# Four weight-tile subtractions of a two-layer hybrid model, on VectorE instead of GpSimd

## The chip, the cores and the metric

The kernel runs on one core of one Trainium2 chip. The core has a tensor engine (TensorE, PE in the profile, with its weight loads as PEld), VectorE (DVE), ScalarE (ACT), GpSimd (POOL) and SyncE (SP), which here issues the DMAs. Each engine works through its own queue in order and waits on semaphores for what the others produce. The metric is device time of one execution in microseconds (us); less is better.

## What is computed

Two layers over 512 tokens of width 1024, batch 1, in fp32. Each layer normalises its input, projects it, mixes it in three ways (a recurrent mix of RWKV type, a gated linear recurrence, and attention on compressed latents), gates the three results and adds their projection to the residual. A norm closes the whole.

```python
h = x
for l in range(DEPTH):                      # 2
    xn = rms_norm(h, ln_g[l])
    proj = xn @ w_in[l]
    u_a, z_a, u_b, z_b, q_lat, kv_lat, k_rope, z_c = jnp.split(proj, pts, axis=-1)
    y_a = rwkv7_mix(u_a, ...)
    y_b = rms_norm(rglru_mix(u_b, ...), lru_out_g[l])
    y_c = rms_norm(mla_mix(q_lat, kv_lat, k_rope, ...), mla_out_g[l])
    y = jnp.concatenate([y_a * silu(z_a), y_b * silu(z_b), y_c * silu(z_c)], axis=-1)
    h = h + y @ w_out[l]
return rms_norm(h, final_g)
```

## The kernel before

**Products in three parts.** A product of fp32 matrices is made of three products of numbers that TensorE takes in one pass (type fp32r). Each operand is split into a high part H, which is a copy rounded to fp32r, and a low part L, which is the operand less H. `mm3` (lines 232 to 234) then adds up H times H, L times H and H times L. So every tile of weights passes through `weights` (L217): a DMA brings it into a `wr` buffer (three of them), ScalarE copies it to H (`wH`, four buffers; the copy is in the helper at L141), and one engine subtracts to give L (`wL`, four buffers; L228). L228 reads two operands from SBUF, `wr` and `wH`. A `wr` buffer is free for the next load when its subtraction is done.

**Which engine subtracts.** A counter `wn` goes up by one per weight tile, over the whole kernel. VectorE takes the tile when the counter divides by `wmod`, GpSimd takes all others. `wmod` is set stage by stage: 5 at the head of a layer (WD, L491), then 1000, 2 and 2. In the first layer the tiles numbered 1 to 4 therefore go to GpSimd, and number 5 to VectorE.

**What the first four tiles are.** The projection's columns are cut into 29 blocks of 128, and a block's weights come in two halves of 128x512. The first product of a layer is block 12, the second block 0, and both are made in two halves of 256 tokens each, so that the first half can start before all rows are normalised (`proj` with `halves`, L330). Tiles 1 and 2 are the halves of block 12, tiles 3 and 4 those of block 0. The raw data of the first three is loaded ahead by the list `LO` (L64); the fourth takes the `wr` buffer that the first leaves.

**The norm beside it.** At the start, four tiles of 128 rows are normalised (`norm_tile`, L287). For each: ScalarE squares and sums the rows (L241), VectorE adds the two sums (L245), ScalarE takes the logarithm and the exponential for a first inverse root (L138), and VectorE refines it in three small steps on 128x1 operands (L253, L254, L255). Then for each half of the columns VectorE scales rows and gains (L297), TensorE transposes four blocks into PSUM (L302), ScalarE copies them out as the high part xH (L141), and VectorE subtracts for the low part xL (L305). The first products need xH and xL of row tiles 0 and 1.

**What sets the order.** The queues' order is not written out: a planner goes through the traced instructions, simulates the engines, and gives each engine the earliest traced instruction that is ready. The norm of all four row tiles is traced ahead of the weights of block 12. Two things are fixed by hand: the list `behind` (L1101) puts the copies to H of tiles 1 and 2 behind the last xH copy of row tile 0, and those of tiles 3 and 4 behind that of row tile 1; and three small VectorE operations (L1104 to L1106) come behind the last xL.

Later in a layer, L498 mixes each projected block with its shifted self, L552 and L562 belong to the chain of decays of the recurrent mix (L562 once for each of four column groups), L524 and L525 are the sums over heads in it, L285 and L300 are the norm's steps in the second layer, and L508 splits two small weights on GpSimd.

Of the kernel before, what the change touches and what calls it, by code (L numbers as in the profile page):

```python
# [12 lines left out]
ALU = mybir.AluOpType  # L13
# [34 lines left out]
def body(ctx, tc, x, wc, wl, wo, w2a2, gagx, wuq, wukv, vec, ln_g, fin_g, cst, out, depth=DEPTH):  # L48
    nc = tc.nc
    V, A, G = nc.vector, nc.scalar, nc.gpsimd  # L50
# [17 lines left out]
    def tl(tag, shape, dt=F32, bufs=1):  # L68
        cnt[0] += 1
        return SB.tile(list(shape), dt, tag=tag, name=f"{tag}_{cnt[0]}", bufs=bufs)  # L70
# [69 lines left out]
    def copy(out, in_, **kw):  # L140
        i = A.activation(out=out, in_=in_, func=AF.Copy, **kw)  # L141
        return getattr(i, "ins", i)
# [63 lines left out]
    def f(ap):  # L206
        return ap.bitcast(F32)
# [6 lines left out]
    wn = [0]  # L214
    wmod = [4]

    def weights(src, n=512, raw=None):  # L217

        if raw is None:
            raw = tl("wr", [128, n], F32, bufs=3)  # L220
            nc.sync.dma_start(out=raw, in_=src)
        H = tl("wH", [128, n], F32R, bufs=4)
        L = tl("wL", [128, n], F32R, bufs=4)
        wn[0] += 1
        i = copy(H, raw)
        if behind:
            tc.add_manual_dep(i, behind.pop(0).name, NOSYNC, reason="issue order")
        (V if wn[0] % wmod[0] == 0 else G).tensor_tensor(out=L, in0=raw, in1=f(H), op=ALU.subtract)  # L228
        return H, L

    def mm3(o, a, b, start, stop):
# [88 lines left out]
    def one_layer(l):  # L320
# [9 lines left out]
        def proj(j, halves=False):  # L330

            if halves:
                o = acc()
                W = [weights(wc[l, j, :, 4 * hf:4 * hf + 4, :].rearrange("p k c -> p (k c)"), raw=raws.pop((j, hf), None)) for hf in range(2)]
                for th in range(2):
                    t = slice(th * 256, (th + 1) * 256)
                    for k in range(8):
                        s = slice((k % 4) * 128, (k % 4 + 1) * 128)
                        w = W[k // 4]
                        mm3(o[:, t], (w[0][:, s], w[1][:, s]), (xH[:, k, t], xL[:, k, t]), k == 0, k == 7)  # L340
                return o
            o, parts = proj_parts(j)
            for part in parts:
                part()
            return o

        def proj_parts(j):
            o = acc()

            def part(hf):  # L350
                H, L = weights(wc[l, j, :, 4 * hf:4 * hf + 4, :].rearrange("p k c -> p (k c)"))
                for k in range(4):
                    s = slice(k * 128, (k + 1) * 128)
                    kk = 4 * hf + k
                    mm3(o, (H[:, s], L[:, s]), xk(kk), kk == 0, kk == 7)

            return o, [lambda: part(0), lambda: part(1)]
# [33 lines left out]
        def out_steps(m, y):  # L391

            W, os = {}, {}

            def step(n, tt, k):
                if tt == 0 and k == 0:
                    W[n] = [weights(wo[l, m, n, :, i, :]) for i in range(4)]
                if k == 0:
                    os[n, tt] = tl("hp", [128, 512], bufs=3), acc()
                    nc.sync.dma_start(out=os[n, tt][0], in_=hsrc[tt, n])  # L400
                hp, o = os[n, tt]
                c = slice(tt * 128, (tt + 1) * 128)
                mm3(o, (y[k][:, 0, c], y[k][:, 1, c]), W[n][k], k == 0, k == 3)
                if k == 3:
                    V.tensor_tensor(out=hp, in0=o, in1=hp, op=ALU.add)
                    hd = spill()
                    nc.sync.dma_start(out=hd, in_=hp)
                    hsrc[tt, n] = hd

            return [lambda n=n, tt=tt, k=k: step(n, tt, k) for n in range(2) for tt in range(4) for k in range(4)]  # L410
# [792 lines left out]
```

## Time and profile before

| | |
|---|---|
| median of 3 runs | 873.0 us (871.79, 873.0, 875.05) |
| the profiled execution | 871.72 us |
| its span in the profile | 869.9 us |
| mean granted TensorE clock | 0.972 of full speed |
| PE, PEld busy | 808.5 us (93%), 624.9 us |
| DVE, ACT, POOL busy | 575.0 us, 493.7 us, 336.1 us |
| DMA | 91.05 MB, mean 105 GB/s |

The span is what the profile covers; the 1.8 us between it and the execution's time lie around it. In rows of the chain of waits a line reads: start in us, duration in us, engine, what is written, line. The chain is followed back from the last instruction, at each step to what released it. In rows of the timeline there follow the operation, output<-input, partitions x elements and type, and the count where like instructions are merged into one row; in brackets stands how long the engine was idle before it and what ended that. In the window table each row is a stretch of the span: its edges and width, then busy time (and instructions) of PE, PEld, DVE, ACT and POOL, the granted clock, the DMA engines' mean share and GB/s. A busy PE is not a PE at its peak, since the ends of matmuls are modelled.

### The profile page before, as it was taken

Reading aid. Unit: us, or ns where it says so; the run is one execution under the profiler, and the core shown is the slowest. Engines: PE = TensorE matmul, PEld = TensorE weight load, DVE = VectorE, ACT = ScalarE, POOL = GpSimd, SP = SyncE. Lnnn points to the kernel's source line nnn. Section 1 sums busy time; section 2 is a strip of 40 time slices with the busy share of each in tenths; the row PEclk is TensorE's granted clock in tenths of the full one; section 3 lists DMA queues with packets and bytes.
Section 4 is the critical chain, followed back from the end, with each engine's and each line's share of the span. In section 5 each row is a group of like instructions: output and inputs, shape, how many; then the busy total and the mean of one; then the engine's idle time right before and its main releaser. Section 6 shows DMA issues by size and latency. Waiting matters only on the chain.

```text
span 869.9 us, 14682 instructions
## 1 busy us (share of the span) xinstructions
PE 808.5 (93%) x5440; PEld 624.9 (72%) x5440; DVE 575.0 (66%) x1169; ACT 493.7 (57%) x980; POOL 336.1 (39%) x303
## 2 busy tenths in 40 slices
PE   3998999998989988999989999999979999899995
PEld 3877878876768867566778788888756787675674
DVE  5687666933656795865484876695265778777736
ACT  5657776356454535564466677844745445365635
POOL 2345357634343342010534656574243423310123
PEclk9997999999899999999989999999999999899998
DMA  6311232420212365213653232333010224731354
GB/s 217 116 62 56 79 108 98 139 75 16 59 33 72 111 215 184 73 57 114 223 177 98 73 98 85 109 108 105 26 42 23 65 86 155 233 109 49 109 170 158
DMA packets 49753, 91.05 MB, mean 105 GB/s; under 512 B 5520, under 2 KB 8336, under 8 KB 49680
## 3 DMA queue, kind: packets, MB, share of 16 engines
q1 hardware_dynamic: 49104, 89.05, 31.8%
q10 hardware_dynamic: 576, 1.05, 0.3%
q8 instruction: 43, 0.70, 0.3%
q14 instruction: 30, 0.25, 0.1%
HBM read 73.30 MB, written 16.78 MB: 104 GB/s over the span
## 4 chain that ended last, share of the span: by engine, by line
PE 70%; DVE 12%; ACT 6%; DMA 4%; issue 4%; POOL 2%; SPq 0%; ACTq 0%; DVEq 0%; POOLq 0%
PE acc L232 16%; PE acc L234 15%; PE acc L233 15%; PE acc L1035 4%; PE ck L1061 3%; PE ps L1053 2%; ACT g L138 2%; PE ps L686 2%; PE ck L827 2%; PE ps L610 1%; ACT UV L141 1%; PE ps L628 1%; DMA dr<-hp 1%; POOL g L701 1%; DMA hp<-in_x_dram 1%
## 5 line engine op out<-in xcount | busy, mean ns | idle before, releaser
L228 POOL TENSOR_TENSOR wL<-wr,wH 128x512 fp32r<-128x512 f32 (+1 forms) x130 | 176.1, 1359 | 296.6 <-ACT wH L141 288.1
L141 ACT ACTIVATE wH<-wr 128x512 fp32r<-128x512 f32 (+1 forms) x192 | 118.9, 622 | 138.9 <-PE acc L233 81.0
L232 PE MATMUL acc<-xH,wH 128*128 128x512 f32 (+1 forms) x496 | 193.5, 391 | 0.0
L234 PE MATMUL acc<-xH,wL 128*128 128x512 f32 (+1 forms) x496 | 192.1, 387 | 0.0
L233 PE MATMUL acc<-xL,wH 128*128 128x512 f32 (+1 forms) x496 | 190.4, 384 | 0.1
L232 PEld LDWEIGHTS acc<-xH,wH 128*128 128x128 f32 x496 | 95.7, 193 | 20.8 <-issue 3.2
L233 PEld LDWEIGHTS acc<-xL,wH 128*128 128x128 f32 x496 | 95.7, 193 | 17.5 <-DVE xL L305 0.6
L234 PEld LDWEIGHTS acc<-xH,wL 128*128 128x128 f32 x496 | 95.3, 192 | 18.0
L232 PE MATMUL acc<-wH,c 128*128 128x512 f32 x192 | 82.7, 431 | 4.2 <-DVE hp L427 4.2
L228 DVE TENSOR_TENSOR wL<-wr,wH 128x512 fp32r<-128x512 f32 (+1 forms) x62 | 51.8, 835 | 50.5 <-ACT wH L141 48.6
L233 PE MATMUL acc<-wL,c 128*128 128x512 f32 x192 | 77.1, 402 | 0.2 <-DVE wL L228 0.2
L234 PE MATMUL acc<-wH,c 128*128 128x512 f32 x192 | 76.4, 400 | 0.0
L141 ACT ACTIVATE UV<-ps 128x512 f32<-128x512 f32 (+4 forms) x88 | 39.3, 478 | 31.0 <-PE ps L1053 22.4
L232 PEld LDWEIGHTS acc<-wH,c 128*128 128x128 f32 x192 | 36.4, 190 | 15.2 <-ACT c L141 3.0
L138 ACT ACTIVATE g<-g 128x512 f32<-128x512 f32 (+1 forms) x58 | 36.4, 628 | 17.5 <-DVE g L704 15.6
L138 ACT ACTIVATE c<-acc,sm 128x128 f32<-128x128 f32 (+3 forms) x64 | 33.5, 526 | 19.3 <-DVE sm L1037 19.1
L1035 PE MATMUL acc<-am,am 128*128 128x128 f32 (+3 forms) x128 | 42.3, 447 | 0.9 <-ACT c L138 0.8
L233 PEld LDWEIGHTS acc<-wL,c 128*128 128x128 f32 x192 | 36.6, 191 | 8.3 <-issue 1.4
L234 PEld LDWEIGHTS acc<-wH,c 128*128 128x128 f32 x192 | 36.5, 190 | 8.4 <-issue 0.5
L141 ACT ACTIVATE c<-g 128x512 fp32r<-128x512 f32 (+1 forms) x40 | 24.3, 628 | 28.9 <-DVE g L958 26.0
L136 ACT ACT_TABLE_LOAD x29 | 37.2, 1283 | 1.2 <-PEq L1191 0.7
L368 POOL TENSOR_TENSOR g<-g,g 128x512 f32<-128x512 f32 x24 | 33.0, 1377 | 12.5 <-ACT g L138 12.5
(217 smaller groups left out, 1602.0 us busy)
## 6 DMA issues: line engine op xcount, KB each, us to landing
wr<-in_wc_dram SPq DMA_DIRECT2D x116, 256.0 KB, 2.7
wr<-in_wo_dram SPq DMA_DIRECT2D x48, 256.0 KB, 3.5
hp<-dr SPq DMA_DIRECT2D x40, 256.0 KB, 3.1
dr<-hp SPq DMA_DIRECT2D x32, 256.0 KB, 3.2
dr<-g SPq DMA_DIRECT2D x16, 256.0 KB, 2.4
g<-dr SPq DMA_DIRECT2D x16, 256.0 KB, 3.6
wr<-in_wl_dram SPq DMA_DIRECT2D x16, 208.0 KB, 2.5
c<-in_x_dram SPq DMA_DIRECT2D x8, 256.0 KB, 6.6
```

The costliest lines, as they stand in the source:

```text
L136: chained(A.preload_act_table_set(SETS[st]))
L138: chained(A.activation(out=out, in_=in_, func=func, **kw))
L141: i = A.activation(out=out, in_=in_, func=AF.Copy, **kw)
L228: (V if wn[0] % wmod[0] == 0 else G).tensor_tensor(out=L, in0=raw, in1=f(H), op=ALU.subtract)
L232: PE.matmul(o, a[0], b[0], start=start, stop=False)
L233: PE.matmul(o, a[0], b[1], start=False, stop=False)
L234: PE.matmul(o, a[1], b[0], start=False, stop=stop)
L368: G.tensor_tensor(out=z, in0=z, in1=s, op=ALU.mult)
L686: PE.matmul(o[hr, :], gw[hr, w, j, :], xc[hr, :], start=True, stop=True)
L827: PE.matmul(to[ur, e, p, :], inv["T"][ur, p * 8 + e * 4 + cp, :], r, start=True, stop=True)
L1035: PE.matmul(o[:, 0:n], qT[:, hd, qt * 128:n], K2[:, p, e, 0:n], start=True, stop=True)
L1061: i = PE.matmul(ot[e * 64:(e + 1) * 64, k2 * 128:T], Vt[:, k2, 2 * p + e, :], PT[:, 2 * (k2 % 2) + e, 0:(4 - k2) * 128], start=(k2 == 0), ...
```

## The change

One condition is added in `weights`: the tiles numbered 1 to 4 are subtracted on VectorE. From the fifth on the rule is as before, and the counter runs on through the second layer, so no other tile changes its engine. The operation, its operands and the rest of the trace are the same.

```diff
         i = copy(H, raw)
         if behind:
             tc.add_manual_dep(i, behind.pop(0).name, NOSYNC, reason="issue order")
-        (V if wn[0] % wmod[0] == 0 else G).tensor_tensor(out=L, in0=raw, in1=f(H), op=ALU.subtract)
+
+        (V if wn[0] % wmod[0] == 0 or wn[0] <= 4 else G).tensor_tensor(out=L, in0=raw, in1=f(H), op=ALU.subtract)
         return H, L
```

## The prediction

> **What bounds the kernel now.** I read the page first, then the chain of waits from 12 to 35 us, then the timeline of GpSimd and VectorE over the same stretch, because the change touches only four instructions there. The page gives the size and shows that the differences on GpSimd are the costliest group by busy time.
>
> ```profile
> span 869.9 us, 14682 instructions
> ...
> L228 POOL TENSOR_TENSOR wL<-wr,wH 128x512 fp32r<-128x512 f32 (+1 forms) x130 | 176.1, 1359 | 296.6 <-ACT wH L141 288.1
> ```
>
> The chain that ended last, while rows 128 to 255 (tile 1) and 256 to 383 (tile 2) are normalised (start, duration):
>
> ```profile
> 12.60 1.25 DVE sm L255
> 13.87 1.72 DVE g L297
> ...
> 19.03 1.27 DVE sm L253
> 20.32 1.21 DVE sm L254
> 21.56 0.17 DVE sm L255
> 21.75 0.76 DVE g L297
> ```
>
> See that L255 on a 128x1 operand takes 1.25 us at 12.60 and 0.17 us at 21.56. The timeline says what stood beside the slow ones: the four differences that the change moves, in two pairs.
>
> ```profile
> 12.54 2.49 POOL L228 TENSOR_TENSOR wL<-wr,wH 128x512 fp32r<-128x512 f32 x2 [11.09 <-ACT wH L141]
> 18.99 2.52 POOL L228 TENSOR_TENSOR wL<-wr,wH 128x512 fp32r<-128x512 f32 x2 [3.96 <-ACT wH L141]
> 29.39 2.61 POOL L508 TENSOR_TENSOR c<-g,c 128x512 fp32r<-128x512 f32 x2 [7.89 <-ACT c L141]
> ```
>
> The first pair ends at about 13.79 and 15.03, the second at about 20.25 and 21.51. VectorE's L255 ends at 13.85, and its first L297 at 15.59, 0.56 after the pair; L253 and L254 end at 20.30 and 21.53. So each slow VectorE instruction waits for a GpSimd difference. Between 15.03 and 29.39 the second pair is all that GpSimd does.
>
> From 22 us on the tensor engine is what ends last (window table: width, busy PE, PEld, DVE, ACT, POOL, granted clock, DMA share, GB/s):
>
> ```profile
> 22.00:28.00 6.00, 5.35 (x45) 5.22 (x45) 4.42 (x11) 3.24 (x6) 0.00 (x0) 1.00 0.45 144
> 28.00:50.00 22.00, 21.99 (x119) 18.56 (x118) 13.24 (x17) 15.18 (x26) 10.67 (x13) 1.00 0.30 97
> ```
>
> It is full from 22.65 to 50, so whatever moment it gets going at is handed down.
>
> **What is removed.** Four stalls on the chain. The clean step of a small operation is 21.56 to 21.75, 0.19 us, and the clean first L297 is the 0.76 segment. The sum: L255 from 12.60 to 13.87 is 1.27, less 0.19, 1.08; the first L297 1.72 less 0.76, 0.96; L253 19.03 to 20.32 is 1.29, less 0.19, 1.10; L254 20.32 to 21.56, 1.24 less 0.19, 1.05. Tile 1 gets 2.04 us, tile 2 2.15 us, together 4.19 us. GpSimd loses 5.0 us of work that nobody else there waits for; its next job, at 29.39, waits for ScalarE.
>
> **What is added.** Four instructions on VectorE, of 0.68 us by the row of 449.22 below. Where they stand in its queue isn't in the trace of before, since the order is a planner's. The nearest rows are in the second layer's norm, where one difference is already on VectorE:
>
> ```profile
> 448.41 0.15 DVE L254 SCALAR_TENSOR_TENSOR sm<-sm,sm 128x1 f32<-128x1 f32 x1
> 448.48 0.68 DVE L285 TENSOR_TENSOR g<-c,c 128x512 f32<-128x512 f32 x1
> 449.08 0.15 DVE L255 SCALAR_TENSOR_TENSOR sm<-sm,sm 128x1 f32<-128x1 f32 x1
> 449.15 0.15 DVE L245 SCALAR_TENSOR_TENSOR sm<-sm 128x1 f32<-128x1 f32 x1
> 449.22 0.68 DVE L228 TENSOR_TENSOR wL<-wr,wH 128x512 fp32r<-128x512 f32 x1
> 449.82 0.87 DVE L300 TENSOR_SCALAR g<-g,sm 128x512 f32<-128x512 f32 x2
> ```
>
> An instruction that is ready is put between two that hang on one another (L285 between L254 and L255, L228 between L255 and L300). L254 to L255 then takes 0.67 instead of 0.19: **an exposed difference costs 0.48 us**. Below it is nothing, where it falls into a wait. The other end is all four exposed, 1.92 us.
>
> When is each ready? ScalarE's copies wH, which they read:
>
> ```profile
> 11.85 1.27 ACT L141 ACTIVATE wH<-wr 128x512 fp32r<-128x512 f32 x2
> ...
> 18.29 0.62 ACT L141 ACTIVATE wH<-wr 128x512 fp32r<-128x512 f32 x1
> ...
> 18.90 0.62 ACT L141 ACTIVATE wH<-wr 128x512 fp32r<-128x512 f32 x1
> ```
>
> The first is ready at 12.48, before L255 would end (12.60 + 0.19 = 12.79): I take it as exposed, behind L255. The second is ready at 13.12, when both L297 (independent of one another) stand ahead of it; it then falls into VectorE's wait for the transposes, free. The third and fourth are ready as tile 2's L253 and L254 run: both exposed.
>
> **The sum.** Tile 1: 2.04 - 0.48 = 1.56 us earlier; so are its transposes, its xH and the first product, which was at 17.50:
>
> ```profile
> 17.50 0.58 PE L232 MATMUL acc<-xH,wH 128*128 128x256 f32 x1
> ...
> 21.38 0.41 PE L232 MATMUL acc<-xH,wH 128*128 128x256 f32 x1
> 21.59 0.33 PE L233 MATMUL acc<-xL,wH 128*128 128x256 f32 x1
> 22.65 0.63 PE L302 MATMUL ps<-C,g 128*128 128x128 f32 x4 [0.72 <-DVE g L297]
> ```
>
> Tile 2: its transposes could start 1.56 + 2.15 - 0.96 = 2.75 us earlier, at 19.90. But 17 products stand ahead of them in the tensor engine's queue, from 17.50 to 21.92. These end 1.56 earlier, at 20.36. So the products become what is late, the idle 0.72 us goes, and the transposes move by 1.56 + 0.72 = **2.3 us**. Two exposed differences in tile 2 are thus covered by 0.46 us of products; if that cover went, the figure is at most 2.75. Bounds from the ordering alone: with the second difference exposed too, 1.80; with the first free too, 2.04 + 0.72 = 2.76.
>
> Behind 22.65 nothing of the norm is changed, and the engine stays full, so I carry 2.3 us to the end. Buffers: freeing a wr buffer lets the next weight load go.
>
> ```profile
> 13.84 8.02 SPq L221 DMA_DIRECT2D wr<-in_wc_dram  x4
> ```
>
> The first of these feeds the fourth copy, wH at 18.90. The first difference now ends at about 13.5 (12.79 + 0.07 + 0.6), against 13.79, so that load isn't later. The second load follows the second difference, which may end later than now; it feeds the fifth copy, behind all of this, and I price it at nothing: the cover is the third and fourth tile's work up to 28 us. The w2a2 loads queue behind the fourth on SyncE and come earlier with it.
>
> The profiled execution took 871.72 us, span 869.9, so by the sum 869.4. It is 1.28 us under the median, 873.0; the forecast in the median's terms is **870.7 us**. A measurement of this kernel tells about 0.5% (4.4 us) from no change, so this is a small gain that counts as the same.
>
> **Rivals.**
>
> *The half-rate products stay where they are.* Products of 256 columns start 0.21 us apart up to 21.59 (rows above) and take 0.12 us of the chain later:
>
> ```profile
> 23.94 0.12 PE acc L232
> ```
>
> The rate doubles between, though the granted clock in the table stands at 1.00; the last before the wait is already shorter, 0.33 us against 0.41, so I put the change at about 21.8. If it does so at the same moment after the change, the work from 20.36 to 21.8 runs at half rate and 0.7 us is given back: 1.6 us, **871.4**. If it comes well earlier, the products give way to the transposes' 2.75 us. The Trainium skill, page "TensorE: Matmul & The Clock Gate", Part 1, says that the window of some 3.4 us that decides the rate is free-running and doesn't start with the work. By that rule the moment moves by none or a whole window, so it is this rival or its reverse, never an even shift; one execution can't show that. I give this rival 0.14.
>
> *The layer's later gap closes.* Compare the same L562 step in both layers, with the gap on the tensor engine ahead of it and the clock behind it:
>
> ```profile
> 67.16 0.50 PE L524 MATMUL ps<-c,bones 128*128 128x512 f32 x1 [2.65 <-ACT c L141]
> ...
> 491.98 0.49 PE L524 MATMUL ps<-c,bones 128*128 128x512 f32 x1 [0.54 <-ACT c L141]
> ```
>
> ```profile
> 68.74 0.69 DVE L562 TENSOR_SCALAR c<-ps 128x512 f32<-128x512 f32 x1 [0.59 <-PE ps L525]
> ...
> 98.59 0.69 DVE L562 TENSOR_SCALAR c<-ps 128x512 f32<-128x512 f32 x1
> ...
> 493.60 0.69 DVE L562 TENSOR_SCALAR c<-ps 128x512 f32<-128x512 f32 x1 [0.59 <-PE ps L525]
> ...
> 518.86 0.69 DVE L562 TENSOR_SCALAR c<-ps 128x512 f32<-128x512 f32 x1
> ```
>
> ```profile
> 68.00:99.00 31.00, 30.80 (x145) 25.47 (x146) 20.85 (x28) 20.88 (x35) 14.93 (x19) 0.83 0.22 73
> 493.00:519.00 26.00, 25.90 (x143) 21.41 (x144) 20.50 (x29) 20.50 (x34) 14.19 (x18) 1.00 0.29 91
> ```
>
> Behind a gap of 2.65 us the step takes 29.85 us at clock 0.83; behind one of 0.54 us, 25.26 at 1.00. If the first gap is shortened or falls so that the clock holds, 4.6 us more are gained: 6.9 us, **866.1**. For it: so little decides. Against it: what makes the gap, a long VectorE chain, moves along whole. 0.16.
>
> *Slower: the second layer gets that gap too.* The four instructions change what the planner sees, and it could put other work into VectorE's chain ahead of 491.98. It takes some 2 us there (three exposed instructions of 0.68) to bring 0.54 to 2.65; the point lies between these. Price: the 2.1 us and the 4.6 us of clock, less 2.3: 4.4 us slower, **877.4**. For it: the first layer has such a gap. Against it: no difference of the second layer changes its engine. 0.11.
>
> *The change doesn't do what it says.* The planner sets the tile's transposes behind more products, or the differences ahead of L305, and the stalls come back as waits for ScalarE: nothing is left, **873.0**. Against it stand the rows of 448.41 to 449.82. 0.09.
>
> **How the numbers follow.** Forecast 0.50 (1.8 to 2.8 us gained, 870.2 to 871.2 by the median), half rate 0.14, gap closes 0.16, second gap 0.11, nothing left 0.09. The runs of before lie from 1.2 under to 2.05 over their median, which widens each case. The range, 866.0 to 875.5, holds all but the slower rival and the lower half of the faster one, 0.19. Faster by over 0.5% is the closed gap, 0.16; slower the second gap, 0.11; the rest, 0.73, is within.
>
> **What would show it.** No VectorE instruction of 1.2 us on 128x1 between 12 and 22 us; four L228 of about 0.68 us on VectorE there, of which three stand between dependent steps; the first 256-column product at about 15.9; the second transposes at about 20.4 without idle time ahead of them; L562 at about 66.4 for 68.74. It is wrong if the differences collect ahead of L297 or L305, if the products wait for wL, or if L562 shifts by other than the transposes did.

## The result, and the profile after

| | before | after |
|---|---|---|
| median of 9 runs each | 873.32 us (871.76 to 877.95) | 869.25 us (864.89 to 871.28) |
| the profiled execution | 871.72 us | 869.25 us |
| its span | 869.9 us | 867.4 us |

The ratio of after to before is 0.9942, with a 95% interval of 0.9917 to 0.9967: 2.9 to 7.2 us faster. The profiled execution is 2.5 us shorter. The forecast was 870.7 us, a ratio of 0.9974, just outside that interval; a repeat below, 0.998, takes it in again.

The lines of the changed kernel are numbered one higher from L229 on. Its page, the span and the two groups of differences (the columns are busy us, mean ns of one, idle time before):

```profile
span 867.4 us, 14685 instructions
...
L229 POOL TENSOR_TENSOR wL<-wr,wH 128x512 fp32r<-128x512 f32 (+1 forms) x126 | 172.5, 1373 | 280.2 <-ACT wH L141 254.0
...
L229 DVE TENSOR_TENSOR wL<-wr,wH 128x512 fp32r<-128x512 f32 (+1 forms) x66 | 54.9, 831 | 50.3 <-ACT wH L141 48.9
```

GpSimd has 126 differences for 130. VectorE in the timeline while rows of tiles 1 and 2 are normalised:

```profile
11.75 0.68 DVE L306 TENSOR_TENSOR xL<-ps,xH 128x512 fp32r<-128x512 f32 x1
12.35 0.15 DVE L256 SCALAR_TENSOR_TENSOR sm<-sm,sm 128x1 f32<-128x1 f32 x1
12.42 0.68 DVE L229 TENSOR_TENSOR wL<-wr,wH 128x512 fp32r<-128x512 f32 x1
13.02 1.41 DVE L298 SCALAR_TENSOR_TENSOR g<-c,sm,c 128x512 f32<-128x512 f32 x2
14.35 0.68 DVE L229 TENSOR_TENSOR wL<-wr,wH 128x512 fp32r<-128x512 f32 x1
...
17.21 0.16 DVE L254 TENSOR_TENSOR sm<-sm 128x1 f32<-128x1 f32 x1
17.29 0.69 DVE L229 TENSOR_TENSOR wL<-wr,wH 128x512 fp32r<-128x512 f32 x1
17.89 0.15 DVE L255 SCALAR_TENSOR_TENSOR sm<-sm,sm 128x1 f32<-128x1 f32 x1
17.96 0.69 DVE L229 TENSOR_TENSOR wL<-wr,wH 128x512 fp32r<-128x512 f32 x1
18.57 0.15 DVE L256 SCALAR_TENSOR_TENSOR sm<-sm,sm 128x1 f32<-128x1 f32 x1
18.75 1.41 DVE L298 SCALAR_TENSOR_TENSOR g<-c,sm,c 128x512 f32<-128x512 f32 x2
```

No small operation takes 1.2 us any more here. Three differences stand between dependent steps, the second in a free place, as forecast. The tensor engine in the timeline (idle time ahead and its cause in brackets):

```profile
15.68 0.58 PE L233 MATMUL acc<-xH,wH 128*128 128x256 f32 x1
...
18.71 0.33 PE L235 MATMUL acc<-xH,wL 128*128 128x256 f32 x1
18.87 0.28 PE L233 MATMUL acc<-xH,wH 128*128 128x256 f32 x1
...
20.42 0.60 PE L303 MATMUL ps<-C,g 128*128 128x128 f32 x4
...
24.36 1.29 PE L303 MATMUL ps<-C,g 128*128 128x128 f32 x8 [0.16 <-DVE g L298]
...
26.40 0.39 PE L234 MATMUL acc<-xL,wH 128*128 128x256 f32 x1 [0.22 <-DVE xL L306]
...
64.65 0.49 PE L525 MATMUL ps<-c,bones 128*128 128x512 f32 x1 [2.64 <-ACT c L141]
```

The first product is at 15.68 for 17.50, tile 2's transposes at 20.42 for 22.65 and without idle time ahead. The products shorten at 18.71. The later gap of 2.64 us is as it was. The next marks on VectorE, the clamps of the first layer's first two column groups, and the windows of the head's start and of that step:

```profile
66.22 0.69 DVE L563 TENSOR_SCALAR c<-ps 128x512 f32<-128x512 f32 x1 [0.59 <-PE ps L526]
...
96.11 0.69 DVE L563 TENSOR_SCALAR c<-ps 128x512 f32<-128x512 f32 x1
```

```profile
12.00:22.00 10.00, 7.95 (x47) 7.45 (x48) 7.78 (x18) 6.75 (x18) 0.00 (x0) 1.00 0.65 223
66.00:96.00 30.00, 30.00 (x140) 24.83 (x140) 20.09 (x26) 19.88 (x33) 13.97 (x19) 0.83 0.24 71
```

**How marks are compared.** The load of the rows lands a little earlier or later in each execution. So below, "the head" is the time from tile 0's second xL (11.75 here, 12.00 before) to the first clamp, which I call mark A (66.22 here, 68.74 before). The head was 56.74 us before and is 54.47 us now: **2.27 us gained**. From mark A to the next clamp it is 29.89 us, before 29.85.

One thing disturbs mark A. The half clock behind the later gap sets in at 66.59 here, just behind the mark; in six runs (`first_two`, `last_two`, `both_engines`, `pool_too`, `held_back`, `order_front`) it sets in 0.7 to 2.6 us ahead of it, and the 1.57 us from the gap's end to mark A become 1.84 to 1.88. So a second mark, G, is used beside it: the product that ends the gap (64.65 here, 67.16 before), counted from tile 0's second xL as well. It is 52.90 us here and 55.16 before: 2.26 us gained.

**Why the total says less than the marks.** Take two long stretches into which no edit below puts work, and from which none takes any, but for `decay_late`, which puts work into the first: from the first layer's third clamp to the second layer's second clamp, and from there to the end of the span.

| execution | mark A | third clamp | clamp in layer 2 | span | the two stretches |
|---|---|---|---|---|---|
| before | 68.74 | 121.23 | 493.60 | 869.9 | 372.37, 376.3 |
| after | 66.22 | 118.74 | 492.89 | 867.4 | 374.15, 374.5 |
| `again` | 66.30 | 118.83 | 492.19 | 867.3 | 373.36, 375.1 |
| `order_front` | 66.52 | 119.73 | 491.66 | 865.9 | 371.93, 374.2 |
| `decay_early` | 67.74 | 115.64 | 487.03 | 864.3 | 371.39, 377.3 |

Each stretch differs by some 3 us between these executions (by 0.6 and 0.8 us between the two of the changed kernel), more than the head gained. Of the 2.49 us that stand at the third clamp, 0.71 are left in layer 2, and the end has 2.5 again.

### The profile page after: what moved, and what is told of

The parts are those of the page before. It is cut to its first block, busy times and chain, and to the rows that moved or that the text cites. A ratio compares the mean times of both kernels' runs of the same rounds, so it can differ in the third digit from the quotient of the medians.

```text
span 867.4 us, 14685 instructions
## 1 busy us (share of the span) xinstructions
PE 806.4 (93%) x5440; PEld 623.4 (72%) x5440; DVE 573.4 (66%) x1173; ACT 493.4 (57%) x980; POOL 331.4 (38%) x299
## 4 chain that ended last, share of the span: by engine, by line
PE 69%; DVE 13%; ACT 7%; issue 4%; DMA 3%; POOL 2%; SPq 1%; ACTq 0%; DVEq 0%; POOLq 0%
PE acc L233 16%; PE acc L235 15%; PE acc L234 15%; PE acc L1036 4%; PE ck L1062 3%; PE ps L1054 2%; ACT g L138 2%; PE ps L687 2%; PE ck L828 2%; PE ps L611 1%; ACT UV L141 1%; POOL g L710 1%; PE ps L629 1%; DMA hp<-dr 1%; POOL g L702 1%
## 5 line engine op out<-in xcount | busy, mean ns | idle before, releaser
L229 POOL TENSOR_TENSOR wL<-wr,wH 128x512 fp32r<-128x512 f32 (+1 forms) x126 | 172.5, 1373 | 280.2 <-ACT wH L141 254.0
L229 DVE TENSOR_TENSOR wL<-wr,wH 128x512 fp32r<-128x512 f32 (+1 forms) x66 | 54.9, 831 | 50.3 <-ACT wH L141 48.9
L138 ACT ACTIVATE c<-acc,sm 128x128 f32<-128x128 f32 (+3 forms) x64 | 33.6, 527 | 19.0 <-DVE sm L1038 18.8
```

The lines of the kernel that those rows point to most:

```text
L138: chained(A.activation(out=out, in_=in_, func=func, **kw))
L229: (V if wn[0] % wmod[0] == 0 or wn[0] <= 4 else G).tensor_tensor(out=L, in0=raw, in1=f(H), op=ALU.subtract)
```

## The experiments

My theory: small VectorE operations stood still beside GpSimd's differences; with the stalls gone the head is 2.3 us shorter, and nothing else changes. The rivals: the gain is GpSimd's idle time or the order of the tensor engine's queue, not the stalls; or what was measured beyond 2.3 us comes from the clock behind mark A. Each run is compared with runs of before on the same chip, made at the same time.

### `again`: the changed kernel once more

The same file, with no edit.

> The changed kernel once more, to see whether the time beyond the head's gain is its own. Mark A is the start of the second clamp of the decay chain (L562 before at 68.74 us, L563 here at 66.22 in the first profile). Stalls alone: mark A again at 66.2 (66.0 to 66.5), the time 2.3 to 2.5 us under before, ratio about 0.997, and what lies beyond that differs from execution to execution in stretches at half clock. A gain of its own beyond the head: ratio 0.994 again, with a stretch in the trace that is shorter than before each time.

868.95 us, ratio 0.998 (0.9958 to 1.0001). Head 54.47 us, first product 15.77, transposes 20.48. The head repeats to the hundredth (in both executions the products happened to double their rate at 18.8 us), the ratio doesn't: before had a median of 873.32 us in the first comparison and 871.58 beside this run.

### `first_two` and `last_two`: half of the change each

```diff
-        (V if wn[0] % wmod[0] == 0 or wn[0] <= 4 else G).tensor_tensor(out=L, in0=raw, in1=f(H), op=ALU.subtract)
+        (V if wn[0] % wmod[0] == 0 or wn[0] <= 2 else G).tensor_tensor(out=L, in0=raw, in1=f(H), op=ALU.subtract)
```

> Only tiles 1 and 2 on VectorE, 3 and 4 on GpSimd again. Stalls alone: no stall in row tile 1 (first 256-column product near 15.7 to 15.9 us), but L254 and L255 of row tile 2 take 1.2 us each again; transposes of row tile 2 at about 21.1 (before 22.65, changed 20.42); mark A at about 67.2. If only the sooner differences count (0.68 for 1.27 us) and not the stalls: mark A close to 66.2, since tiles 1 and 2 are the ones that the first products wait for.

870.19 us, ratio 0.9979 (0.9955 to 1.0004). The timeline, all engines, of `first_two`:

```profile
17.22 2.53 POOL L229 TENSOR_TENSOR wL<-wr,wH 128x512 fp32r<-128x512 f32 x2 [15.75 <-ACT wH L141]
...
17.26 1.25 DVE L254 TENSOR_TENSOR sm<-sm 128x1 f32<-128x1 f32 x1
18.55 1.22 DVE L255 SCALAR_TENSOR_TENSOR sm<-sm,sm 128x1 f32<-128x1 f32 x1
...
20.89 0.63 PE L303 MATMUL ps<-C,g 128*128 128x128 f32 x4 [1.37 <-DVE g L298]
```

Tile 1 is clean, tile 2 has its stalls back, one for each difference on GpSimd, and the tensor engine waits 1.37 us for it. The head is 55.47 us, 1.27 less than before. Up to G it is 53.60 us, 1.56 less, which is what the first product gained (3.93 for 5.50 us behind tile 0's second xL).

```diff
-        (V if wn[0] % wmod[0] == 0 or wn[0] <= 4 else G).tensor_tensor(out=L, in0=raw, in1=f(H), op=ALU.subtract)
+        (V if wn[0] % wmod[0] == 0 or 3 <= wn[0] <= 4 else G).tensor_tensor(out=L, in0=raw, in1=f(H), op=ALU.subtract)
```

> Only tiles 3 and 4 on VectorE, 1 and 2 on GpSimd again. Stalls alone: row tile 1 is as before (first product near 17.4, L256 1.2 us), row tile 2 has no stall, the idle 0.72 us ahead of its transposes goes: mark A at about 68.0. The parts then don't add up to more than the whole: 1.5 and 0.7 make 2.2 to 2.3. If the differences' lateness counts: no change against before, 68.7, since no product waits for tiles 3 and 4.

870.56 us, ratio 1.0001 (0.998 to 1.0023). The timeline of `last_two`:

```profile
11.71 1.24 DVE L256 SCALAR_TENSOR_TENSOR sm<-sm,sm 128x1 f32<-128x1 f32 x1
...
21.15 0.32 PE L233 MATMUL acc<-xH,wH 128*128 128x256 f32 x1
...
22.02 0.60 PE L303 MATMUL ps<-C,g 128*128 128x128 f32 x4
```

A miss. The second half alone gains nothing: up to G it takes 55.15 us, before 55.16 (the head, 57.02 us, is 0.28 more, for the half clock sets in ahead of mark A). I had expected the idle 0.72 us ahead of the transposes to go. It went, but 25 products now stand ahead of them instead of 17, and until 21.15 these run at half rate, so the transposes end up no earlier than they were (10.91 us behind tile 0's second xL, before 10.65). So the parts don't add up: 1.56 and 0.01 up to G, against 2.26 together. My reading, not tested by a run, is that the half that clears tile 1 lets the products start, and that the other half is worth something only behind it. A part of the difference isn't the edits': the products ran at half rate for 2.8 us in `first_two`, 4.6 in `last_two` and 3.1 in the changed kernel, and that length differs from execution to execution (see the rivals below).

### `both_engines`: the change, and the stalls put back

The four differences stay on VectorE, and GpSimd does each a second time into a scratch tile that nobody reads. The order of VectorE, TensorE, ScalarE and SyncE is that of the changed kernel.

```diff
         (V if wn[0] % wmod[0] == 0 or wn[0] <= 4 else G).tensor_tensor(out=L, in0=raw, in1=f(H), op=ALU.subtract)
+        if wn[0] <= 4:
+            G.tensor_tensor(out=tl("sqn", [128, T]), in0=raw, in1=f(H), op=ALU.subtract)
```

> The changed kernel, and GpSimd makes the same four subtractions besides, into a scratch tile outside the norm's buffers, so that the queues of VectorE and TensorE are those of the changed kernel. Stalls between the two engines are the cause: VectorE's operations in the head take 1.2 us and more beside GpSimd again, the first product comes 1 to 2 us after that of the changed kernel, and mark A (second clamp of the decay chain, 54.5 us behind the second xL of row tile 0 in the changed kernel, 56.7 in the one before) is at 56.5 to 59 us behind it. If the engine or the lateness of the differences counts: 54.3 to 54.8.

873.33 us, ratio 0.9999 (0.9975 to 1.0023). Its timeline:

```profile
13.18 3.00 POOL L231 TENSOR_TENSOR sqn<-wr,wH 128x512 f32<-128x512 f32 x2 [11.72 <-ACT wH L141]
...
13.24 1.23 DVE L258 SCALAR_TENSOR_TENSOR sm<-sm,sm 128x1 f32<-128x1 f32 x1
...
14.99 2.41 DVE L300 SCALAR_TENSOR_TENSOR g<-c,sm,c 128x512 f32<-128x512 f32 x2
...
20.26 1.78 DVE L229 TENSOR_TENSOR wL<-wr,wH 128x512 fp32r<-128x512 f32 x1
...
21.97 1.24 DVE L257 SCALAR_TENSOR_TENSOR sm<-sm,sm 128x1 f32<-128x1 f32 x1
```

The head is 58.39 us, in the range expected: all of the gain is gone, and 1.65 us more (1.35 up to G). With four queues unchanged and only GpSimd's work back, this shows the stalls as the cause. Both sides pay: two differences on GpSimd take 3.00 us here and 2.49 before. L258 ends at 14.47, some 1.29 us after GpSimd's first difference began, and the two L300 at 17.40, 1.22 us after its second ended at 16.18. So one engine waits for the other's whole instruction. The Trainium skill, page "SBUF — State Buffer", section "Who interferes with whom", says that a VectorE instruction with two inputs in SBUF contends with a GpSimd instruction that reads SBUF, because its second input comes through a read interface that the two share. The runs agree with it: L258 has two such inputs and takes 1.23 us, while L309 of `pool_late` below, with one input in PSUM, takes its usual 0.69 us in the middle of a GpSimd difference.

A first try, with the scratch in the norm's `g2` buffers, tells nothing of the stalls: it took up buffers that the head needs, the loads came late and the tensor engine stood idle.

```diff
+        if wn[0] <= 4:
+            G.tensor_tensor(out=g2(), in0=raw, in1=f(H), op=ALU.subtract)
```

> The changed kernel, and GpSimd makes the same four subtractions besides, into a scratch tile that nobody reads. Stalls between the two engines are the cause: the small VectorE operations beside GpSimd take 1.2 us again, and mark A goes from 66.2 to 68.5 to 70. If it is the difference's engine or its lateness that counts: the products get wL from VectorE as in the changed kernel and mark A stays within 0.3 us of 66.2.

873.66 us, ratio 1.0028 (1.0004 to 1.0052), head 58.89 us.

### `held_back`: GpSimd idle, but the head as long as before

Two more 128x512 operations on VectorE, whose results nobody reads, ahead of tile 1's scaling and of tile 2's.

```diff
+        for _ in range(2 if l == 0 and tt in (1, 2) else 0):
+            V.scalar_tensor_tensor(out=g2(), in0=gb[:, 0:512], scalar=rs, in1=gb[:, 512:1024], op0=ALU.mult, op1=ALU.mult)
         for j in range(2):
```

> The changed kernel with two extra 128x512 VectorE operations ahead of L298 in row tiles 1 and 2, 0.7 us each, their result unused; GpSimd does nothing there. If VectorE's time ahead of L298 is all that the change altered: the first product at about 17.1 us, mark A at 68.0 to 68.9, and the time as before (ratio 0.999 to 1.001). If GpSimd being idle is worth something by itself: mark A stays under 67.

871.08 us, ratio 0.999 (0.9968 to 1.0012). The first product is at 17.93, mark A at 68.91, the head 56.24 us, 0.5 less than before (0.75 up to G) and 1.8 more than in the changed kernel. About as expected: once VectorE's chain is nearly as long as it was, taking the work off GpSimd is worth 0.75 us at most.

### `order_back` and `order_front`: the order on TensorE

Outside the moved instructions, the change altered one queue: the planner put tile 2's transposes behind 25 products instead of 17. Both kernels try to set the old order by hand.

```diff
...
-                PE.transpose(p[:, k, :], src[:, k * 128:(k + 1) * 128], ident)
+                i = PE.transpose(p[:, k, :], src[:, k * 128:(k + 1) * 128], ident)
+                trs[l, tt, j] = getattr(i, "ins", i)
...
-                        mm3(o[:, t], (w[0][:, s], w[1][:, s]), (xH[:, k, t], xL[:, k, t]), k == 0, k == 7)
+                        ms = mm3(o[:, t], (w[0][:, s], w[1][:, s]), (xH[:, k, t], xL[:, k, t]), k == 0, k == 7)
+                        if l == 0 and j == 12 and th == 0 and k == 5:
+                            tc.add_manual_dep(ms[2], trs[0, 2, 0].name, NOSYNC, reason="issue order")
+                        if l == 0 and j == 12 and th == 0 and k == 6:
+                            tc.add_manual_dep(ms[0], trs[0, 2, 1].name, NOSYNC, reason="issue order")
```

> The changed kernel with row tile 2's transposes put back behind 17 and 18 of the first products, as in the kernel before (the planner had moved them behind 25 and 26, after the differences were on VectorE). If the planner's move costs part of the gain: these transposes start at about 19.6 to 19.8 us instead of 20.42, mark A (second clamp of the decay chain, 66.22 and 66.30 in the two profiles of the changed kernel) comes at 65.5 to 65.9. If the tensor engine's products bind anyway: both within 0.15 us of the changed kernel.

869.69 us, ratio 0.9974 (0.9956 to 0.9992). It didn't do what it was to do: the planner drew products of block 0 ahead instead, the transposes stayed behind 25 (20.68), and the head is 54.56 us. `order_front` ties those too:

```diff
-                        if l == 0 and j == 12 and th == 0 and k == 6:
+                        if l == 0 and th == 0 and (j, k) in ((12, 6), (0, 0)):
                             tc.add_manual_dep(ms[0], trs[0, 2, 1].name, NOSYNC, reason="issue order")
```

> The changed kernel with row tile 2's transposes held behind 17 and 18 products of the first block, and the other block's products behind them too (in the earlier try the planner had drawn these ahead instead). If the planner's move of the transposes costs part of the gain: they start about 0.7 us sooner behind the second xL of row tile 0 (8.0 for 8.67 us), mark A is at 53.7 to 54.2 us behind it. If the products bind anyway: 54.4 to 54.6.

868.71 us, ratio 0.9964 (0.9938 to 0.999). The timeline of `order_front`:

```profile
19.74 0.41 PE L233 MATMUL acc<-xH,wH 128*128 128x256 f32 x1
...
20.16 0.61 PE L304 MATMUL ps<-C,g 128*128 128x128 f32 x4
```

Now the transposes come at 20.16, 8.23 us after tile 0's second xL, in the changed kernel 8.67. The head is 54.59 us, against 54.47; up to G it is 52.72, against 52.90. So the gain isn't the new order's: with the old one all of it is still there, and the transposes 0.44 us earlier add 0.18 us at G. That the planner's new order costs nothing isn't shown by this: the products ran at half rate for 4.3 us here and 3.1 in the changed kernel, which by their spacing (0.21 us, then 0.12) is some 0.5 us of work, and the waits of 0.16 and 0.22 us at 24.36 and 26.40 aren't there. At equal rates the old order would be some 0.7 us better, an estimate from these figures that no run tests.

### `pool_late`: the differences stay on GpSimd, but later

They are made to wait for the second scaling of the tile, so that they fall where VectorE waits for the transposes.

```diff
...
-        (V if wn[0] % wmod[0] == 0 or wn[0] <= 4 else G).tensor_tensor(out=L, in0=raw, in1=f(H), op=ALU.subtract)
+        i = (V if wn[0] % wmod[0] == 0 else G).tensor_tensor(out=L, in0=raw, in1=f(H), op=ALU.subtract)
+        if wn[0] <= 4:
+            tc.add_manual_dep(getattr(i, "ins", i), scaled[1 if wn[0] <= 2 else 2].name, SYNC, reason="behind the scaling")
...
-                V.scalar_tensor_tensor(out=src, in0=h[tt][:, s], scalar=rs, in1=gb[:, s], op0=ALU.mult, op1=ALU.mult)
+                i = V.scalar_tensor_tensor(out=src, in0=h[tt][:, s], scalar=rs, in1=gb[:, s], op0=ALU.mult, op1=ALU.mult)
+                scaled[tt] = getattr(i, "ins", i)
```

> All four differences on GpSimd, but each pair waits for the second L298 of its row tile (1 and 2), so that GpSimd works while VectorE waits for the transposes. Stalls alone: no small VectorE operation over 0.2 us in the head and nothing put between them, so mark A is 0.4 to 0.8 us ahead of the changed kernel, 65.4 to 65.8. If the gain comes from sooner differences: they end 1.5 to 2 us later than in the kernel before, so mark A is at 68 or later.

869.78 us, ratio 0.9986 (0.9959 to 1.0013). The timeline of `pool_late`:

```profile
14.10 2.51 POOL L229 TENSOR_TENSOR wL<-wr,wH 128x512 fp32r<-128x512 f32 x2 [12.64 <-ACT g L244]
...
15.20 0.69 DVE L309 TENSOR_TENSOR xL<-ps,xH 128x512 fp32r<-128x512 f32 x1 [0.97 <-ACT xH L141]
15.22 0.58 PE L235 MATMUL acc<-xH,wH 128*128 128x256 f32 x1
...
17.14 0.16 DVE L258 SCALAR_TENSOR_TENSOR sm<-sm,sm 128x1 f32<-128x1 f32 x1
17.34 1.41 DVE L300 SCALAR_TENSOR_TENSOR g<-c,sm,c 128x512 f32<-128x512 f32 x2
...
18.88 2.54 POOL L229 TENSOR_TENSOR wL<-wr,wH 128x512 fp32r<-128x512 f32 x2 [2.27 <-ACT wH L141]
```

The norm's steps are as clean as in the changed kernel, without the exposed differences on VectorE. The head is 53.10 us: 1.37 us less than in the changed kernel, where I had expected 0.4 to 0.8. The first product accounts for 0.47 of it (15.22 - 11.76 = 3.46 against 15.68 - 11.75 = 3.93); the rest, tile 2's two exposures gone and full rate from about 17.7 on, I can't separate. The total doesn't show it.

### `decay_late`, `decay_early`, `late_and_early`: the later gap

The rival of the closed gap put 4.6 us on the clock behind it. What makes the gap is a long VectorE chain, and in it stand small operations on 128x8, the decay rates. In the changed kernel's timeline:

```profile
49.12 1.14 DVE L271 TENSOR_TENSOR sm<-sm 128x8 f32<-128x8 f32 x1
...
50.30 1.23 DVE L272 TENSOR_SCALAR sm<-sm 128x8 f32<-128x8 f32 x1
51.56 2.36 DVE L274 SCALAR_TENSOR_TENSOR sm<-sm,sm 128x8 f32<-128x8 f32 x7
```

`ORD1` is the list in which the first layer's jobs are traced; `D0` is that chain. First it goes to the list's end:

```diff
-    ORD1 = "M0 L0 L1 D0 C0 M1 C1 P0 L2 O0 M2 U1 O1 C2 U2 P1 L3 M3 C3 U0 P2 O2"
+    ORD1 = "M0 L0 L1 C0 M1 C1 P0 L2 O0 M2 U1 O1 C2 U2 P1 L3 M3 C3 U0 P2 O2 D0"
```

> The changed kernel with the decay rates (17 small VectorE operations, L266 to L279) at the end of the first stage instead of ahead of the decay chain. If the gap on the tensor engine ahead of mark A (2.64 us) brings on the half clock behind it: the gap falls under 1 us, mark A comes at 63.5 to 64.5, and the step from mark A to the next clamp takes about 25.3 us, as in the second layer, instead of 29.9; in all 6 to 7 us, ratio to the changed kernel 0.992 to 0.993. If the half clock comes from the narrow products behind the gap: mark A at 64, the step still 29.9, about 2 us in all.

869.44 us, ratio 0.9962 (0.9945 to 0.998). The gap and the chain in the timeline of `decay_late`, and its windows:

```profile
62.03 0.49 PE L525 MATMUL ps<-c,bones 128*128 128x512 f32 x1 [0.39 <-ACT c L141]
...
128.45 5.25 DVE L274 SCALAR_TENSOR_TENSOR sm<-sm,sm 128x8 f32<-128x8 f32 x6
```

```profile
64.00:89.00 25.00, 24.96 (x139) 20.67 (x136) 20.82 (x27) 19.43 (x32) 13.68 (x19) 1.00 0.27 87
120.00:150.00 30.00, 26.46 (x132) 21.93 (x131) 24.60 (x49) 15.35 (x26) 18.61 (x16) 0.89 0.27 87
```

With a gap of 0.39 us the clock stays at 1.00 and the step from mark A (63.65) to the next clamp (88.93) takes 25.28 us, not 29.89: 4.6 us, the rival's price to the tenth. The rates' small operations went elsewhere and the narrow products behind the gap stayed, so it was the gap. At the third clamp the kernel is 7.2 us ahead of the changed one (111.57 for 118.74). But the chain has only been moved: at 128 us it stands beside GpSimd again, and the clock falls to 0.89 there. In layer 2 (491.62 for 492.89) 1.3 us are left, and in the total, 869.44 us, nothing shows against the changed kernel's 869.25 and 868.95: the 6 to 7 us expected were missed. So the rates go to a place ahead of the layers, directly behind the norm:

```diff
-    ORD1 = "M0 L0 L1 D0 C0 M1 C1 P0 L2 O0 M2 U1 O1 C2 U2 P1 L3 M3 C3 U0 P2 O2"
+    ORD1 = "M0 L0 L1 C0 M1 C1 P0 L2 O0 M2 U1 O1 C2 U2 P1 L3 M3 C3 U0 P2 O2"
...
+    decay_rates()
     for l in range(depth):
         one_layer(l)
```

> The changed kernel with the decay rates (17 small VectorE operations, one exponential) traced directly behind the norm, where GpSimd is idle. The gap ahead of mark A is what brings on the half clock: gap under 1 us, mark A at 51 to 52.5 us behind the second xL of row tile 0 (54.5), the step to the next clamp 25.3 us for 29.9, no new gap at 115 to 140 us; 6 to 7 us in all, ratio to the kernel before 0.989 to 0.992. If a stall of that kind comes back somewhere else, as with the rates at the stage's end: the step shortens and the time stays at 0.996 to 0.998.

866.42 us (6 runs), ratio 0.9933 (0.9907 to 0.9959). The timeline of `decay_early`:

```profile
29.55 3.58 DVE L274 SCALAR_TENSOR_TENSOR sm<-sm,sm 128x8 f32<-128x8 f32 x7
...
34.47 0.50 PE L235 MATMUL acc<-xH,wL 128*128 128x512 f32 x1 [1.76 <-DVE wL L229]
...
66.13 0.49 PE L525 MATMUL ps<-c,bones 128*128 128x512 f32 x1 [0.40 <-ACT c L141]
```

The step behind mark A is 25.25 us (67.74 to 92.99). The price is a wait of 1.76 us for a difference that VectorE makes late, and the half clock that it brings on, 3.41 us from 35.41 on (a granted clock of 0.50), some 1.7 us of lost work at most. So the head is 55.61 us, where 51 to 52.5 were expected. Third clamp 115.64, 3.1 us ahead of the changed kernel.

`late_and_early` is `pool_late` with `decay_early`:

```diff
...
+        if wn[0] <= 4:
+            tc.add_manual_dep(getattr(i, "ins", i), scaled[1 if wn[0] <= 2 else 2].name, SYNC, reason="behind the scaling")
...
+    decay_rates()
```

> GpSimd's four differences behind the scaling (as in pool_late) and the decay rates directly behind the norm together. If both gains stand by themselves: mark A at 50 to 51.5 us behind the second xL of row tile 0, 8 us under the kernel before, ratio 0.988 to 0.991. If the differences, now later, run into the rates on VectorE: no better than the rates alone.

**863.6 us** (861.03 to 865.09, 6 runs), ratio 0.9904 (0.9878 to 0.9929): the best kernel of the study, ahead of both. Its timeline:

```profile
33.15 0.50 PE L237 MATMUL acc<-xH,wL 128*128 128x512 f32 x1 [1.38 <-DVE wL L229]
...
63.20 0.49 PE L528 MATMUL ps<-c,bones 128*128 128x512 f32 x1 [0.39 <-ACT c L141]
```

Step behind mark A 25.25 us (64.81 to 90.06). The total is in the range expected, the head isn't: 53.22 us for 50 to 51.5, no better than in `pool_late` (53.10), since the wait of 1.38 us and a longer stretch at half rate (4.1 us, in `pool_late` 2.5) eat up what the closed gap gives.

## Why the prediction was right

**What is removed: right.** The four stalls are gone, and `both_engines` brings them back with everything else in place. `first_two` shows that each belongs to its own GpSimd difference.

**Where the four land: right.** First exposed behind L256 (it was L255), second free, third and fourth exposed, each at the forecast price (17.21 to 17.89 is 0.68 us, clean 0.19). The first product comes 3.93 us after tile 0's second xL; the forecast, 15.94 against 12.00, is 3.94.

**What covers tile 2: the same cover, by another route.** The forecast had 17 products at half rate until 20.36, and tile 2's transposes directly behind them. There were 25, and the rate doubled at 18.8. The times look alike (20.42 for 20.36), but the rows landed 0.25 us earlier in this execution: behind tile 0's second xL the transposes come at 8.67 us, forecast 8.36, before 10.65. So they moved by 1.98 us and not by 2.3, with eight more products done ahead of them. That the products, not tile 2's norm, set the pace there holds in both orders: neither trace has idle time ahead of these transposes. That the old order would stay was wrong.

**2.3 us carried to mark A: the number is right, in part by luck.** Up to G, 1.57 us come from the first product. Behind it the idle 0.72 us are gone, as forecast. Two things that the forecast didn't have nearly cancel: a shorter stretch at half rate (3.1 us for 4.2), worth some 0.5 us, and two waits of 0.16 us at 24.36 and 0.22 us at 26.40, when the products have caught up with tile 3's norm, so the engine didn't stay full. That makes some 2.4, measured 2.26. The balance is worked out from the rows, not tested by a run of its own. By one of the prediction's own signs, that the clamp shifts as the transposes do, it is off here: 2.27 us against 1.98. `order_front` is nearer to the case that the forecast describes, with the old order and half rate for 4.3 us, and gains 2.44 us up to G.

**The median: the size is open.** The marks and the span give 2.3 to 2.5 us, the first comparison 2.9 to 7.2 us, the repeat at most 3.7 us (0.9958) and as little as nothing. The medians of before went from 871.34 to 873.32 us over the comparisons. I have no mechanism that adds to the 2.3 us, and whether there is more isn't settled.

**The rivals.** *Half-rate products*: the doubling didn't stay at 21.8, but it wasn't the change that moved it. The half-clock stretches later in a trace all begin on a raster of 3.41 us (the last section shows its rows), and the doubling falls on the same raster: before, 14 sections of it ahead of the stretch at 69.48 (21.7), in the changed kernel 14 ahead of the one at 66.59 (18.8), in `order_front` 13 ahead of 64.55 (20.2). It does so in all 14 traces, to within 0.2 us. Where the raster lies differs from execution to execution, so the half rate lasted from 1.9 us (`decay_late`) to 5.1 us (`pool_too`) behind the first product. The Trainium skill, page "TensorE: Matmul & The Clock Gate", Part 1, says that the window that decides the rate is free-running, and that the moment varies by 500 ns either way for that reason. The traces agree with the first; the scatter is wider than the second. "None or a whole window", as the prediction had it, would need the raster to lie alike in both executions; it was worth some 0.5 us here, in the change's favour. *The later gap*: it moved along whole, as I argued against it; its price is confirmed. *The second layer's gap*: there the wait is 0.56 us for 0.54 before (at 491.30), so nothing came of it. *The change doesn't do what it says*: it does.

## What to carry to other kernels

A tiny VectorE operation costs a whole GpSimd instruction when the two meet (0.16 us became 1.25), so look for GpSimd work beside a chain of small dependent steps, and try that work in the chain's waits before moving it to the engine that is on the path (here the head was 1.37 us shorter so; the total didn't show it). Half of such a change can be worth nothing until the other half is there, so read the parts from marks in the trace and not from totals that scatter by more. A short gap on the tensor engine can cost more through the clock behind it than it lasts: shortening one of 2.6 us to 0.4 brought 4.6 us more in its step, and it paid only where the work that made the gap found a better place.

## What the runs showed of the hardware that was not expected

A single gap of 2.64 us, followed by one product and another wait of 0.55 us, was enough for a stretch at half clock: the step of 25.3 us took 29.9, at a granted clock of 0.83. A gap of 0.39 us at the same place did not do it, in three kernels.

The traces show when it happens. The granted clock changes only on a raster: all 118 half-clock stretches of the 14 traces begin a whole number of sections of 3.413 us from the first of their trace (795.31 us, from the first to the last of the changed kernel, are 233 of them). How busy TensorE was in one section decides nearly always whether the next runs at half clock. The window rows of the changed kernel's section with the gap and of the three behind it, and then the row of the section behind `decay_early`'s wait of 1.76 us:

```profile
63.18:66.59 3.41, 1.40 (x10) 0.85 (x12) 2.00 (x3) 3.38 (x7) 3.41 (x5) 1.00 0.21 77
66.59:76.83 10.24, 10.24 (x47) 8.68 (x44) 7.64 (x13) 6.13 (x10) 2.63 (x5) 0.50 0.19 51
```

```profile
35.41:38.82 3.41, 3.41 (x10) 2.61 (x9) 2.13 (x3) 3.30 (x6) 0.60 (x1) 0.50 0.67 230
```

From 30 us on the 14 traces hold 3259 whole sections at full clock. The 99 of them in which TensorE was busy for less than 1.49 us were all followed by half clock, the 3123 with 1.80 us or more never, and of the 37 between 19 were. So a section need not be idle throughout, and it matters where a gap lies: the 1.76 us in `decay_early` fall into one section (busy 1.65 us), the 1.38 us in `late_and_early` into two (busy 2.42 and 3.04), and there the clock held. The ends of matmuls are modelled, so the two bounds are rough.

The products of the head ran at half rate for 1.9 to 5.1 us (0.41 us each, then 0.28), while the granted clock of the window from 12 to 22 us stands at 1.00.

Chains of tiny operations beside GpSimd are stretched by a simple count: each GpSimd instruction that runs beside them holds up one. Of the seven L274 on 128x8 that took 2.36 us at 51.56 in the changed kernel, one took 1.15 us and six 0.17, beside one GpSimd instruction that began there. In `decay_early`, 3.58 us at 29.55, two took 1.28, beside two. In `decay_late`, 5.25 us for six at 128.45, where GpSimd had work without a pause, four took 1.13 to 1.25, beside four. An operation with a single input in SBUF can be held too: L272, a TENSOR_SCALAR, took 1.23 us at 50.30 beside a GpSimd difference and 0.16 us at 124.67 in `decay_late` without one.
